# Layer 0's output projection turned into features by tokens, with a block-transposed way back for the residual

## The chip, the cores and the metric

The kernel runs on one core of one Trainium2 chip. The core has TensorE (PE in the profile, with its weight loads shown apart as PEld), VectorE (DVE), ScalarE (ACT), GpSimd (POOL) and SyncE (SP). Here SP issues nearly all transfers, and POOL a few. The metric is the device time of one execution in microseconds. The kernel before takes 2053.34 us, the median of three runs (2053.01, 2053.34 and 2054.17 us).

## The reference

The program is a two-layer encoder over 256 tokens of 2048 features, in float32. In each layer 12 mixing heads and 4 heads that look into 256 memory tokens run side by side. Their outputs are concatenated (16 heads of 128, "cat") and go through one output projection, whose result is added to the residual. A squared-ReLU MLP of width 8192 follows. Every sub-layer normalises its input first.

```
h = x
for i in range(DEPTH):
    n = rms_norm(h, attn_norm[i])
    ...
    h = h + jnp.concatenate([mix, cross], axis=-1) @ w_o[i]
    n = rms_norm(h, mlp_norm[i])
    h = h + jnp.square(jax.nn.relu(n @ w_up[i])) @ w_down[i]
return rms_norm(h, final_norm)
```

The change touches the line with `w_o[0]`, and what carries its result into the norm behind it and into the residual.

## The kernel before

**Products.** Every float32 operand is split into a rounded high part and the rest (`split`, L299: ScalarE writes the high part, VectorE the low part), and each product is three TensorE products: high by high, high by low, low by high. There are two forms. In form "S" (`s_products`, L215) a 128x128 block of weights is stationary and the 256 tokens stream past; the result has features on partitions and tokens along the row. In form "M" (`m_products`, L202) 128 tokens of the activation are stationary and 512 columns of weights stream past; the result has tokens on partitions. Layer 0's query and key projections and both up projections (`u_products`, L690) have the first form. The value projections, all of layer 1's input projection and both output projections have the second.

**Weights.** A chunk of weights is 128x2048 (1 MB), loaded by SP into one of three "raw" slots. It is split in two halves into `hi` and `lo` tiles, of which there are four each, so a half can be split once the half four before it has been multiplied. The up projection has its own set on the side: two raw slots (`raw_U`) and two slots each of `uh` and `ul`.

**The output projection** (`add_o`, L674) goes over four blocks of 512 output features. Each needs four chunks, whose rows are heads: 12 to 15 (memory heads), 0 to 3, 4 to 7, 8 to 11. Blocks 0 and 1 are interleaved so that heads 8 to 11, the last to be ready, come last. `o_done` (L603) adds a block to `h` (tokens by features) and sums squares. After three of the four blocks `guard` forms a scale from them, so the up projection need not wait for the full norm; its inverse (`inv`) corrects what the MLP adds to `h`. Then `scaled` (L621) multiplies `h` by the scale, and `transposed` (L314) turns it to features by tokens on TensorE: 32 transposes of 128x128 (L319), each feature tile then split into `hT` (`split_pair`, L324). The up projection multiplies with `hT`.

**Order.** The author writes a list of half-chunks ("grains"). Each has a run, and loads and splits a few grains ahead; `later(n, ...)` puts a piece of work n grains later. The framework then orders the instructions of every engine itself: it takes this order as a priority and goes by its own estimate of when data will be there. The order is fixed when the program is built. Each engine, and SP and POOL as issuers of transfers, then works through its list strictly in order: a row that waits holds up all rows behind it.

Of the kernel before, what the change touches and what calls it, by code (L numbers as in the profile page):

```python
# [57 lines left out]
class Work:  # L58


    def __init__(self, kind, src, acts, first, begins, last, start, done):
        self.kind, self.src, self.acts = kind, src, acts
        self.first, self.begins, self.last, self.start, self.done = first, begins, last, start, done
        self.early = False


# [8 lines left out]
def encoder_kernel(ctx: ExitStack, tc: tile.TileContext, t: dict, out: bass.AP):  # L75
# [69 lines left out]
    def halves_of(w):  # L145
# [9 lines left out]
        def prep(hf):  # L155
            if hf == 0:
                tiles["raw"] = at.ring.tile([P, CH], F32, tag="raw", bufs=3, name="raw")
                nc.sync.dma_start(tiles["raw"], w.src)
            tiles[hf] = new_half(w.kind)
            split(*tiles[hf], tiles["raw"][:, hf * HALF : (hf + 1) * HALF])  # L160
# [54 lines left out]
    def s_products(w, k0, nk, hi, lo):  # L215

        acts, ps = w.acts(), w.ps[:, :SEQ]
        for j in range(nk):
            k = k0 + j
            s = slice(j * P, (j + 1) * P)  # L220
            nc.tensor.matmul(ps, hi[:, s], acts[:, k, :SEQ], start=k == 0, stop=False)  # L221
            nc.tensor.matmul(ps, hi[:, s], acts[:, k, SEQ:], start=False, stop=False)  # L222
            nc.tensor.matmul(ps, lo[:, s], acts[:, k, :SEQ], start=False, stop=k == KT - 1)  # L223

# [121 lines left out]

    def attend(qT, kT, bias=None):
        sc_ps = at.att.tile([P, NT, SEQ], F32, tag="att", name="sc_ps")
# [20 lines left out]
        for s in range(NT):  # L369
            nc.vector.tensor_scalar(sc[:, s, :], sc[:, s, :], rs[:, s : s + 1], None, op0=ALU.mult)  # L370
        return sc
# [18 lines left out]

    def attention(jobs, at, gap=1, lag=1):

        def step(n, job, prev):
            qT, kT, bias, v, head, cat = job
            if n == 0:
                res = attend(qT, kT, bias)
# [120 lines left out]
    def x_stats():  # L517
# [6 lines left out]
        box["x_col"] = keep.tile([P, NT], F32, name="x_col")  # L524
        nc.vector.tensor_copy(box["x_col"], rstd_of(ss, D, "x"))
        box["x_row"] = at.work.tile([P, SEQ], F32, tag="x_row", bufs=1, name="x_row")
        along_free(box["x_col"], box["x_row"])
# [27 lines left out]
    def a_k_done(hd):  # L555
        def f(w):
            k = at.work.tile([P, 512], F32R, tag="b_y2", name="kT")
            s = summed(w.ps, "k", box["x_row"])
            split(k[:, :SEQ], k[:, SEQ:], s)
            b = at.work.tile([P, BJ * GRID_W], F32, tag="b_o", bufs=3, name="bias")  # L560
            nc.sync.dma_start(b, t["bias"][hd])
            attention([(box.pop(("q", hd)), k, b, head_of(box["v", hd // GH], hd % GH), hd, box["cat"])], 1)
        return f

    def a_qm_done(hd):
        def f(w):
# [4 lines left out]
            split(q[:, :SEQ], q[:, SEQ:], s)  # L571
            attention([(q, box["km"][:, hd, :], None, head_of(box["vm"], hd), NH + hd, box["cat"])], 1)
        return f
# [29 lines left out]
    def o_done(layer, nb):  # L603
# [33 lines left out]
        def f(w):  # L637
# [20 lines left out]
            if nb == 3:  # L658
# [7 lines left out]
                later(6, past, squares)  # L666
                later(8, past, inv)
        return f

# [312 lines left out]

    add_o(0)
    add_mlp(0)
# [246 lines left out]
```

## Time and profile before

| | |
|---|---|
| median of three runs | 2053.34 us |
| span of the profiled execution | 2050.6 us |
| median less span | 2.7 us |
| PE busy | 2028.0 us (99%) |
| DVE, ACT busy | 1657.1 us (81%), 1242.0 us (61%) |
| output projection of layer 0 | 347.6 to 440.4 us of the span, its last transposes to 444.4 us |
| up projection of layer 0 begins | 440.5 us |

The page does not state the profiled execution's whole time; its span is compared with the median of the runs. In the rows, a time stamp counts from the span's start. Products overlap, so their durations (0.28 or 0.39 us each) do not add up to time; the distance from one start to the next does.

### The profile page before, as it was taken

To read this page: it belongs to the slowest core of one execution; us is meant where nothing else is said; L and a number is where in the kernel's file an instruction comes from. 1 tells how busy PE (TensorE), PEld (TensorE's weight loads), DVE (VectorE), ACT (ScalarE), POOL (GpSimd) and SP (SyncE) were. 2 spreads that over 40 slices of the span, in tenths; PEclk is the share of its full clock that TensorE was granted. 3 is DMA by queue.
4 is the path that set the end of the run, shared out by engine and by line. 5 is a ranking of instruction groups with operands and counts; after the bars stand their busy time and mean duration, and the time that the engine had idled before them with its cause. 6 is when DMAs were issued, how large, how long until landed. Compare 5 with 4: busy or idle time off the path is not lost.

```text
span 2050.6 us, 32620 instructions
## 1 busy us (share of the span) xinstructions
PE 2028.0 (99%) x13092; PEld 1835.2 (89%) x13092; DVE 1657.1 (81%) x2025; ACT 1242.0 (61%) x1616; POOL 120.2 (6%) x144
## 2 busy tenths in 40 slices
PE   8999999999999999999999999999999999999998
PEld 7899999889999999999988888889999999999996
DVE  6766666558998999989896667657989999999896
ACT  6645454556666666666655557556666666666664
POOL 0000000000000000000000001000000000000000
PEclk9999999999999999999999999999999999999999
DMA  7755555727777777777765554537878787777773
GB/s 280 284 190 180 189 175 178 275 86 224 234 228 232 218 238 230 220 234 226 232 219 204 178 180 144 195 115 224 242 223 237 215 243 220 232 226 228 231 220 134
DMA packets 93431, 433.84 MB, mean 212 GB/s; under 512 B 10464, under 2 KB 12128, under 8 KB 60128
## 3 DMA queue, kind: packets, MB, share of 16 engines
q1 hardware_dynamic: 75888, 399.25, 57.7%
q0 software_dynamic: 16816, 31.46, 8.7%
q8 instruction: 102, 1.67, 0.3%
q10 hardware_dynamic: 576, 1.05, 0.1%
q14 instruction: 49, 0.40, 0.1%
HBM read 398.17 MB, written 4.19 MB: 196 GB/s over the span
## 4 chain that ended last, share of the span: by engine, by line
PE 94%; DVE 3%; DMA 1%; ACT 1%; issue 1%; SPq 0%; POOLq 0%; POOL 0%; DVEq 0%; ACTq 0%
PE ps_u L698 11%; PE ps_u L696 11%; PE ps_u L697 11%; PE p L810 8%; PE p L811 8%; PE p L812 8%; PE ps_m L209 8%; PE ps_m L212 8%; PE ps_m L213 8%; PE ps_s L221 3%; PE ps_s L223 3%; PE ps_s L222 3%; DVE ul L302 1%; PE pt_a L378 1%; DVE tl L302 1%
## 5 line engine op out<-in xcount | busy, mean ns | idle before, releaser
L698 PE MATMUL ps_u<-hT,ul 128*128 128x256 f32 x2048 | 568.1, 278 | 2.4 <-DVE ul L302 2.3
L696 PE MATMUL ps_u<-hT,uh 128*128 128x256 f32 x2048 | 568.0, 277 | 0.1
L697 PE MATMUL ps_u<-hT,uh 128*128 128x256 f32 x2048 | 567.4, 277 | 0.0
L301 ACT ACTIVATE uh<-raw_U 128x1024 fp32r<-128x1024 f32 x278 | 294.6, 1061 | 303.5 <-PE ps_u L697 281.0
L302 DVE TENSOR_TENSOR lo<-raw,hi 128x1024 fp32r<-128x1024 f32 (+1 forms) x224 | 266.3, 1195 | 162.1 <-ACT hi L301 160.0
L698 PEld LDWEIGHTS ps_u<-hT,ul 128*128 128x128 f32 x2048 | 385.5, 188 | 5.2 <-DVE ul L302 4.2
L696 PEld LDWEIGHTS ps_u<-hT,uh 128*128 128x128 f32 x2048 | 384.9, 188 | 5.5 <-ACT uh L301 0.5
L697 PEld LDWEIGHTS ps_u<-hT,uh 128*128 128x128 f32 x2048 | 384.4, 188 | 4.6
L302 DVE TENSOR_TENSOR ul<-raw_U,uh 128x1024 fp32r<-128x1024 f32 x278 | 337.2, 1218 | 37.5 <-ACT uh L301 37.4
L301 ACT ACTIVATE hi<-raw 128x1024 fp32r<-128x1024 f32 (+1 forms) x224 | 231.8, 1040 | 215.9 <-PE ps_m L213 121.1
L301 ACT ACTIVATE th<-t 128x2048 fp32r<-128x2048 f32 x112 | 215.2, 1921 | 125.4 <-PE p L812 111.8
L302 DVE TENSOR_TENSOR tl<-t,th 128x2048 fp32r<-128x2048 f32 x112 | 256.1, 2286 | 26.4 <-ACT th L301 25.8
L302 DVE TENSOR_TENSOR bl<-b,bh 128x1536 fp32r<-128x1536 f32 x112 | 196.0, 1750 | 0.3 <-ACT bh L301 0.2
L811 PE MATMUL p<-tl,a_s 128*128 128x512 f32 x448 | 177.2, 395 | 0.0
L812 PE MATMUL p<-th,a_s 128*128 128x512 f32 x448 | 174.4, 389 | 0.0
L301 ACT ACTIVATE bh<-b 128x1536 fp32r<-128x1536 f32 x112 | 166.2, 1484 | 10.1 <-PE p L812 4.0
L810 PE MATMUL p<-th,a_s 128*128 128x512 f32 x448 | 166.1, 395 | 0.0
L790 POOL DMA_DIRECT2D t<-b x112 | 97.1, 867 | 1166.0 <-DVE t L789 593.6
L811 PE MATMUL p<-bl,a_s 128*128 128x512 f32 x336 | 131.0, 390 | 0.2 <-DVE bl L302 0.2
L812 PE MATMUL p<-bh,a_s 128*128 128x512 f32 x336 | 131.1, 390 | 0.0
L789 DVE TENSOR_TENSOR t<-t,b 128x512 f32<-128x512 f32 x112 | 77.2, 689 | 64.1 <-DMA t<-in_w_pair 52.5
L223 PE MATMUL ps_s<-nT,lo 128*128 128x256 f32 x448 | 124.9, 279 | 0.0
(233 smaller groups left out, 3813.4 us busy)
## 6 DMA issues: line engine op xcount, KB each, us to landing
raw_U<-in_w_up SPq DMA_DIRECT2D x128, 1024.0 KB, 6.6
b<-in_w_pair SPq DMA_DIRECT2D x112, 768.0 KB, 4.5
raw<-in_w_o SPq DMA_DIRECT2D x32, 1024.0 KB, 5.1
t<-in_w_pair SPq DMA_DIRECT2D x112, 256.0 KB, 3.5
t<-b POOLq DMA_DIRECT2D x112, 256.0 KB, 6.8
raw<-in_w_b SPq DMA_DIRECT2D x21, 1024.0 KB, 5.0
raw<-in_w_av SPq DMA_DIRECT2D x12, 1024.0 KB, 5.1
raw<-in_w_aq SPq DMA_DIRECT2D x12, 1024.0 KB, 5.0
```

The costliest lines, as they stand in the source:

```text
L209: first = nc.tensor.matmul(w.ps[i], ah, hi[:, s], start=st, stop=False)
L212: nc.tensor.matmul(w.ps[i], ah, lo[:, s], start=False, stop=False)
L213: nc.tensor.matmul(w.ps[i], al, hi[:, s], start=False, stop=sp)
L223: nc.tensor.matmul(ps, lo[:, s], acts[:, k, :SEQ], start=False, stop=k == KT - 1)
L301: first = nc.scalar.activation(dst_hi, src, AF.Copy)
L302: return first, nc.vector.tensor_tensor(dst_lo, src, dst_hi.bitcast(F32), op=ALU.subtract)
L696: nc.tensor.matmul(ps, hi[:, s], acts[:, k, :SEQ], start=k == 0, stop=False)
L697: nc.tensor.matmul(ps, hi[:, s], acts[:, k, SEQ:], start=False, stop=False)
L698: nc.tensor.matmul(ps, lo[:, s], acts[:, k, :SEQ], start=False, stop=k == KT - 1)
L810: nc.tensor.matmul(ps, a[:, 0, ai, :], hi[:, s], start=begins, stop=False)
L811: nc.tensor.matmul(ps, a[:, 0, ai, :], lo[:, s], start=False, stop=False)
L812: nc.tensor.matmul(ps, a[:, 1, ai, :], hi[:, s], start=False, stop=ends)
```

## The change

Layer 0's output projection becomes form S (`add_o_still`): 16 works, one per tile of 128 output features, each with one chunk of weights `w_os` whose 16 blocks are in the order of heads 12 to 15, 0 to 11. The first four works are interleaved: their four first halves, then their four second halves. The result has features on partitions, as the up projection needs it.

The scale now comes from the input instead of three blocks of `h`: the probabilities of all layer 0 heads are multiplied by the reciprocal root of the mean square of `x` of their token (`factor`, an extra operand of an instruction that is there already), so `cat` carries it, and the projection's result comes out scaled. `rows` loads `x` once more, features by tokens (four loads of 512 KB, `x_s`), and multiplies it by the same scale. For each feature tile VectorE adds the two into `room`, and `split_pair` makes `hT` of it.

`h` itself has to be tokens by features for the MLP's additions. For every pair of feature tiles `back` transposes 32x32 blocks on VectorE (one instruction for 128x512), writes them to DRAM in four transfers on SP (64 KB each, `turn`), and reads them back in one transfer on POOL (256 KB). Five grains later `landed` copies them on ScalarE into `h`, times the inverse scale, and after every second pair sums the squares.

Besides, `raw` has four slots for three, and the framework's scratch memory for transfers issued by POOL is set to 8192.

```diff
-    raws = [at.ring.tile([P, CH], F32, tag="raw", bufs=3, name=f"raw{c}") for c in range(FIRST_CHUNKS)]
+    raws = [at.ring.tile([P, CH], F32, tag="raw", bufs=4, name=f"raw{c}") for c in range(FIRST_CHUNKS)]
...
+                nc.vector.tensor_scalar(sc[:, s, :], sc[:, s, :], rs[:, s : s + 1], factor[:, i : i + 1],
+                                        op0=ALU.mult, op1=ALU.mult)
...
+    def add_o_still(layer):
+
+        heads = [*range(NH, KT), *range(NH)]
+        works = []
+        for n in range(KT):
+            def start(w):
+                w.ps = at.acc.tile([P, 512], F32, tag="acc", name="ps_s")
+            works.append(Work("S", t["w_os"][n], get("cat"), 0, True, True, start, o_still_done(layer, n)))
+            works[-1].kts = heads
+        first = [halves_of(w) for w in works[:4]]
+        for hf in range(2):
+            plan.extend(x[hf] for x in first)
+        plan.extend(works[4:])
+
+    def o_still_done(layer, n):
+
+        def back():
+            room = box["room"]
+            x, y, z = (room[:, i, :] for i in range(3))
+            nc.vector.transpose(y.rearrange("p (b i d r) -> p d i b r", b=4, i=2, d=2),
+                                x.rearrange("p (d i b j) -> p d i b j", d=2, i=2, b=4))
+            f = P
+            turn = dram.tile([P, 4, f], F32, tag="turn", bufs=4, name="turn")
+            to = turn.rearrange("(b r) a f -> a r b f", r=32)
+            for a in range(4):
+                nc.sync.dma_start(to[a], y.rearrange("p (b f) -> p b f", b=4)[32 * a : 32 * a + 32])
+            z = z.rearrange("p (a f) -> p a f", a=4)
+            nc.gpsimd.dma_start(z, turn)
+            later(5, landed, z, n // 2)
+
+        def landed(z, pair):
+            src = z.rearrange("p a (i d r) -> p i d a r", i=2, d=2)
+            for i in range(NT):
+                dst = h[:, i, pair * 256 : (pair + 1) * 256].rearrange("p (d a r) -> p d a r", d=2, a=4)
+                nc.scalar.activation(dst, src[:, i], AF.Copy, scale=box["x_root"][:, i : i + 1])
+            if pair % 2:
+                for i in range(NT):
+                    sum_squares(2 * layer, i, pair // 2)
+            if pair == KT // 2 - 1:
+                inv()
...
+        def rows(q):
+            x = at.side.tile([P, 3 * 512], F32, tag="b", bufs=2, name="x_s")[:, : 4 * SEQ]
+            nc.sync.dma_start(x, t["xT"][:, q * 4 * SEQ : (q + 1) * 4 * SEQ])
+            x = x.rearrange("p (a b) -> p a b", b=SEQ)
+            nc.vector.tensor_tensor(x, x, box["x_row"][:, None, :].to_broadcast([P, 4, SEQ]), op=ALU.mult)
+            box["x_s", q] = x
+
+        def f(w):
+            if n == 0:
+                closed("work")
+                at.side = opened("side", side="right")
+                box["hT"] = wide(f"hT{layer}")
+                rows(0)
+            if n % 4 == 0 and n < 12:
+                rows(n // 4 + 1)
+            if n % 2 == 0:
+                box["room"] = at.side.tile([P, 4, 512], F32, tag="T", bufs=2, name="room")
+            x = box["room"][:, 0, n % 2 * SEQ : n % 2 * SEQ + SEQ]
+            nc.vector.tensor_tensor(x, w.ps[:, :SEQ], box["x_s", n // 4][:, n % 4, :], op=ALU.add)
+            split_pair(box["hT"], x, (G_M0, G_M1)[layer], n)
+            if n % 2:
+                back()
+        return f
...
-    add_o(0)
+    add_o_still(0)
...
-    nc = _bacc.Bacc("TRN2", target_bir_lowering=False, num_devices=1)
+    nc = _bacc.Bacc("TRN2", target_bir_lowering=False, num_devices=1, dynamic_dma_scratch_size=8192)
```

**How the order moves.** Line numbers in the changed program are those of the changed file (L223 to L225 are the three products of form S, L303 and L304 the two parts of `split`). On PE, as the second halves of the first four works begin to end, the changed program has these rows. `ps_s_3876`, `3915`, `3953` and `3982` are the sums of works 0 to 3, and `hi_3949`, `hi_3978`, `hi_4007` and `hi_4050` are the high parts of their second halves:

```order
L224 MATMUL ps_s_3982<-cat0_1142,hi_4050 128x256
L223 MATMUL ps_s_3876<-cat0_1142,hi_3949 128x256
L223 MATMUL ps_s_3915<-cat0_1142,hi_3978 128x256
L223 MATMUL ps_s_3953<-cat0_1142,hi_4007 128x256
L225 MATMUL ps_s_3982<-cat0_1142,lo_4051 128x256
L223 MATMUL ps_s_3982<-cat0_1142,hi_4050 128x256
L224 MATMUL ps_s_3876<-cat0_1142,hi_3949 128x256
L225 MATMUL ps_s_3876<-cat0_1142,lo_3950 128x256
L224 MATMUL ps_s_3915<-cat0_1142,hi_3978 128x256
L225 MATMUL ps_s_3915<-cat0_1142,lo_3979 128x256
L224 MATMUL ps_s_3953<-cat0_1142,hi_4007 128x256
```

The last three products of works 0, 1 and 2, those of head 11, stand behind five products of work 3's second half; until then the sums and the weight tiles of all three stay in use. VectorE has, in that stretch, the following rows. The first row holds the low parts of the second halves of works 2 and 3, and the later `lo` rows are the halves of work 4:

```order
L304 TENSOR_TENSOR lo<-raw,hi 128x1024 x2
L304 TENSOR_TENSOR pT<-pt_a,pT 128x512
L304 TENSOR_TENSOR cat_1142<-av,cat_1142 128x256
L736 TENSOR_TENSOR x_s<-x_s,x_row 128x1024
L750 TENSOR_TENSOR room<-ps_s,x_s 128x256 x3
L736 TENSOR_TENSOR x_s<-x_s,x_row 128x1024
L304 TENSOR_TENSOR lo<-raw,hi 128x1024
L702 STREAM_TRANSPOSE room<-room 128x2x2x4x32
L304 TENSOR_TENSOR lo<-raw,hi 128x1024
```

Both multiplications of `x_s`, and three additions that wait for head 11, stand ahead of the split of work 4's first half. At the other end, where the up projection of layer 0 begins, ScalarE had these rows before:

```order
L301 ACTIVATE uh<-raw_U 128x1024
L327 ACTIVATE hT_4327<-pt_n,gains 128x256 x4
L586 ACTIVATE sq,ssq_114<-h 128x512
L301 ACTIVATE uh<-raw_U 128x1024
L586 ACTIVATE sq,ssq_114<-h 128x512
L301 ACTIVATE uh<-raw_U 128x1024
L750 ACTIVATE c<-ps_u 128x256
```

In the changed program it has these, where the first row of L717 is the sixth of `landed` counted from zero (features 1536 to 1791), the second is the last, and `uh` rows are halves of up chunks 1, 1, 2 and 2:

```order
L329 ACTIVATE hT_4039<-room,gains 128x256 x2
L717 ACTIVATE h<-room,x_root 128x256 x2
L329 ACTIVATE hT_4039<-room,gains 128x256
L303 ACTIVATE uh<-raw_U 128x1024 x2
L836 ACTIVATE c<-ps_u 128x256
L837 ACTIVATE c<-c 128x256
L717 ACTIVATE h<-room,x_root 128x256 x2
L599 ACTIVATE sq,ssq_114<-h 128x512
L303 ACTIVATE uh<-raw_U 128x1024
L599 ACTIVATE sq,ssq_114<-h 128x512
L303 ACTIVATE uh<-raw_U 128x1024
```

The copy of the last pair back into `h`, which reads a transfer from DRAM, now stands ahead of the split of up chunk 2. SP, the issuer, has at that place:

```order
L159 DMA raw<-in_w_os 128x2048
L861 DMA b<-in_w_pair 128x1536
L708 DMA turn<-room 32x4x128 x8
L863 DMA t<-in_w_pair 128x512
L861 DMA b<-in_w_pair 128x1536
L708 DMA turn<-room 32x4x128 x4
L794 DMA raw_U<-in_w_up 128x2048
L863 DMA t<-in_w_pair 128x512
L794 DMA raw_U<-in_w_up 128x2048 x5
```

The four writes of the last pair stand behind the MLP's first load `t`, which takes the memory of the sixth pair's `room` and so waits until that pair has been copied into `h`. Before, SP had two `t` and six `raw_U` in a row there, and no writes.

More of the change, by code (lines that the diff above doesn't have):

```diff
@@ L64, in __init__ @@
         self.early = False
+        self.kts = range(KT)
 class Grain:
@@ L156, in prep @@
             if hf == 0:
-                tiles["raw"] = at.ring.tile([P, CH], F32, tag="raw", bufs=3, name="raw")
+                tiles["raw"] = at.ring.tile([P, CH], F32, tag="raw", bufs=4, name="raw")
                 nc.sync.dma_start(tiles["raw"], w.src)
@@ L369, in attend @@
         for s in range(NT):
-            nc.vector.tensor_scalar(sc[:, s, :], sc[:, s, :], rs[:, s : s + 1], None, op0=ALU.mult)
+            if factor is None:
+                nc.vector.tensor_scalar(sc[:, s, :], sc[:, s, :], rs[:, s : s + 1], None, op0=ALU.mult)
+            else:
+                i = NT - 1 - s
+                nc.vector.tensor_scalar(sc[:, s, :], sc[:, s, :], rs[:, s : s + 1], factor[:, i : i + 1],
+                                        op0=ALU.mult, op1=ALU.mult)
         return sc
@@ L389, in attend3, with attention @@
         split(cat[:, head, :SEQ], cat[:, head, SEQ:], av[:, :SEQ])
-    def attention(jobs, at, gap=1, lag=1):
+    def attention(jobs, at, gap=1, lag=1, factor=None):
         def step(n, job, prev):
@@ L395, in step @@
             if n == 0:
-                res = attend(qT, kT, bias)
+                res = attend(qT, kT, bias, factor)
             elif n == 1:
@@ L524, in x_stats @@
         box["x_col"] = keep.tile([P, NT], F32, name="x_col")
-        nc.vector.tensor_copy(box["x_col"], rstd_of(ss, D, "x"))
-        box["x_row"] = at.work.tile([P, SEQ], F32, tag="x_row", bufs=1, name="x_row")
+        box["x_mean"] = keep.tile([P, NT], F32, name="x_mean")
+        nc.vector.tensor_scalar(box["x_mean"], ss, 1.0 / D, EPS, op0=ALU.mult, op1=ALU.add)
+        nc.gpsimd.tensor_tensor(box["x_col"], box["x_mean"], mhalf[:, :NT], op=ALU.pow)
+        box["x_root"] = keep.tile([P, NT], F32, name="x_root")
+        nc.vector.tensor_tensor(box["x_root"], box["x_mean"], box["x_col"], op=ALU.mult)
+        box["x_row"] = keep.tile([P, SEQ], F32, name="x_row")
         along_free(box["x_col"], box["x_row"])
@@ L561, in f @@
             nc.sync.dma_start(b, t["bias"][hd])
-            attention([(box.pop(("q", hd)), k, b, head_of(box["v", hd // GH], hd % GH), hd, box["cat"])], 1)
+            attention([(box.pop(("q", hd)), k, b, head_of(box["v", hd // GH], hd % GH), hd, box["cat"])], 1,
+                      factor=box["x_col"])
         return f
@@ L571, in f @@
             split(q[:, :SEQ], q[:, SEQ:], s)
-            attention([(q, box["km"][:, hd, :], None, head_of(box["vm"], hd), NH + hd, box["cat"])], 1)
+            attention([(q, box["km"][:, hd, :], None, head_of(box["vm"], hd), NH + hd, box["cat"])], 1,
+                      factor=box["x_col"])
         return f
@@ new lines, in o_still_done, with inv @@
+    def o_still_done(layer, n):
[22 more added lines that the diff above has]
+                inv()
+        def inv():
+            v = mean_square(2 * layer, 4, "full")
+            box["inv"] = keep.tile([P, NT], F32, tag="inv", name="inv")
+            nc.vector.reciprocal(v, v)
+            nc.vector.tensor_tensor(box["inv"], v, box["x_mean"], op=ALU.mult)
+            box["ninv"] = keep.tile([P, NT], F32, tag="ninv", name="ninv")
+            nc.vector.tensor_scalar(box["ninv"], box["inv"], -1.0, None, op0=ALU.mult)
+        def rows(q):
[19 more added lines that the diff above has]
+                back()
@@ L1214 @@
         arrays[f"w_vm{i}"] = m_chunks(a["w_mem_kv"][i][:, memw:])
-        arrays[f"w_o{i}"] = m_chunks(a["w_o"][i])
+        if i == 0:
+            rows = a["w_o"][i].reshape(KT, HD, D)
+            arrays["w_os"] = s_chunks(np.concatenate([rows[NH:], rows[:NH]]).reshape(D, D))
+        else:
+            arrays[f"w_o{i}"] = m_chunks(a["w_o"][i])
         arrays[f"w_up{i}"] = s_chunks(a["w_up"][i])
```

9 lines of the change are left out of this document (5 added, 4 removed).

## The prediction

> **What bounds the kernel now.** I read the page's engine shares first, then the stretches of the span around the projection and the start of the MLP, then who TensorE waited for there.
>
> ```profile
> PE 2028.0 (99%) x13092; PEld 1835.2 (89%) x13092; DVE 1657.1 (81%) x2025; ACT 1242.0 (61%) x1616; POOL 120.2 (6%) x144
> 347.00:450.00 103.00, 102.95 (x521) 87.28 (x519) 57.41 (x72) 53.53 (x81) 0.69 (x1) 1.00 0.49 181
> 447.00:451.00 4.00, 3.45 (x28) 3.05 (x27) 2.85 (x5) 2.85 (x7) 0.00 (x0) 1.00 0.01 2
> 451.00:475.00 24.00, 23.69 (x208) 23.69 (x209) 15.45 (x26) 14.16 (x21) 0.00 (x0) 1.00 0.57 188
> 475.00:490.00 15.00, 13.63 (x112) 13.02 (x111) 13.51 (x17) 11.29 (x14) 1.93 (x2) 1.00 0.81 245
> PE ps_u L698 <- DVE ul L302: 1.1, 2, 0.8
> 448.95 1.06 ACT uh L301
> 450.03 1.24 DVE ul L302
> ```
>
> In a row of stretches the numbers are the length, then the busy time of PE, PEld, DVE, ACT and POOL, then the granted clock. TensorE has no free time in the projection (102.95 of 103.00 us), at full clock. VectorE (57.4) and ScalarE (53.5) have nearly half of it free. So only two things can move the time: how long TensorE's own list is, and waits that the new rows put into it. Before, it waits 0.8 us at the first split of up chunk 1's second half (the chain shows `uh`, then `ul`), and 1.4 us (15.00 less 13.63) where the first down products begin. The second belongs to code that the change leaves.
>
> **TensorE's list.** The same multiplications in the two forms:
>
> ```profile
> 343.04 0.28 PE L223 MATMUL ps_s<-nT,lo 128*128 128x256 f32 x1
> ...
> 347.46 0.28 PE L223 MATMUL ps_s<-nT,lo 128*128 128x256 f32 x1
> 400.14 0.39 PE L212 MATMUL ps_m<-lo,cat 128*128 128x512 f32 x1
> ...
> 402.86 0.39 PE L213 MATMUL ps_m<-hi,cat 128*128 128x512 f32 x1
> 425.01 0.22 PE pt_n L319 x2
> 425.47 1.53 PE pt_n L319 x14
> 435.42 0.87 PE pt_n L319 x8
> 442.59 0.22 PE pt_n L319 x2
> 443.75 0.66 PE pt_n L319 x6
> ```
>
> From 343.04 to 347.46 us lie 39 products of form S: 0.1133 us each. From 400.14 to 402.86 lie 12 of form M: 0.2267 us. Form M has 16 k-blocks x 2 token tiles x 4 feature blocks x 3 = 384 products, 87.0 us. Form S has 16 x 16 x 3 = 768, also 87.0 us. **That term is zero.** What goes is the 32 transposes: the five rows of the chain add up to **3.5 us**. The 26 small products of heads 10 and 11 that fall into the stage stay.
>
> **Start of the stage.** Count from A, the first product of the projection. A half is 24 products, 2.72 us. The small products are spaced about 0.12 us:
>
> ```profile
> 353.94 0.28 PE L386 MATMUL av<-pT,va 128*128 128x256 f32 x1
> 355.61 0.39 PE L209 MATMUL ps_m<-hi,cat 128*128 128x512 f32 x1
> L302 DVE TENSOR_TENSOR lo<-raw,hi 128x1024 fp32r<-128x1024 f32 x30 | 36.6, 1224 | 28.5 <-ACT hi L301 28.4
> L301 ACT ACTIVATE hi<-raw 128x1024 fp32r<-128x1024 f32 x29 | 30.7, 1060 | 32.4 <-PE ps_m L213 28.0 <-PE ps_s L222 1.7 <-issue 1.4
> L343 DVE SCALAR_TENSOR_TENSOR k_s<-ps_s,x_row 128x256 f32<-128x256 f32 x1 | 0.4, 425 | 0.5 <-PE ps_s L223 0.5
> ```
>
> (14 pieces in 1.67 us there, so 26 take 3.1 us.) By the order on PE, works 0 to 2 end after 4x24 + 3x21 + 5 + about 3 = 167 products: A + 18.9 + 3.1 = A + 22.0. Work 4 is due 25 products later, A + 24.9, and needs its low part two products on, A + 25.1. From A + 22.0 VectorE has three additions (3 x 0.425), one multiplication of `x_s` (128x1024, 1.22 as a split of that size) and the split (1.22): A + 25.7, **0.6 us late** even with all data there. The first `x_s` stands on SP behind the eighth weight chunk, whose slot is free when the low part of work 3's second half is split: work 3's first half ends at A + 13.7 (96 products and most of the small ones), plus 1.06 and 1.22, A + 16.0.
>
> ```profile
> raw<-in_w_o SPq DMA_DIRECT2D x3, 1024.0 KB, 5.0
> raw<-in_w_o SPq DMA_DIRECT2D x5, 1024.0 KB, 8.4
> t<-in_w_pair SPq DMA_DIRECT2D x1, 256.0 KB, 3.2
> 380.00:390.00 10.00, 10.00 (x46) 8.28 (x45) 5.94 (x6) 4.82 (x6) 0.00 (x0) 1.00 1.01 406
> ```
>
> The chunk lands 5.0 us later, at A + 21.0, and 0.5 MB behind it at 406 GB/s takes 1.3 more: A + 22.3. Then 1.22 + 1.28 + 1.22 + 1.22 end at A + 27.2, 2.1 us late. With an uncrowded 3.2 us it stays 0.6; with the crowded chunk of 8.4 us it is 5.5. I take **1.5**, since the nearest row (5.0) points to 2.1 and smaller transfers to 0.6.
>
> **The way back.** For each pair: a transpose (nearest row: an addition of 128x512, 0.69), four issues, a write, a return on POOL, two copies.
>
> ```profile
> L789 DVE TENSOR_TENSOR t<-t,b x3: 685/685/692, 475.3 to 494.0; 128x512 f32<-128x512 f32 x3
> 375.03 0.33 SPq L158 DMA_DIRECT2D raw<-in_w_o  x1
> gains<-in_gains SPq DMA_DIRECT2D x1, 40.0 KB, 1.9
> mem_k<-km_w SPq DMA_DIRECT2D x4, 256.0 KB, 9.6
> t<-b POOLq DMA_DIRECT2D x1, 256.0 KB, 3.7
> t<-b POOLq DMA_DIRECT2D x112, 256.0 KB, 6.8
> L586 ACT ACTIVATE sq<-h 128x512 bf16<-128x512 f32 x8 | 5.0, 624 | 3.1 <-DVE h L644 3.1
> L586 ACT ACTIVATION_READ_ACCUMULATOR sq<-h 128x1 f32 x7 | 1.3, 187 | 0.0
> ```
>
> A write of 64 KB lies between 1.9 (40 KB) and 9.6 (256 KB into DRAM in a crowded stretch); I take 2.3, near the small one, for no weights are moving then. The return lies between 3.7 and 6.8; I take 3.7, the one of the quiet stretch. From the transpose's start that is 0.7 + 4x0.33 + 2.3 + 3.7 = 8.0 us. For pairs 0 to 6 this is hidden: weights are split three halves (8.2 us) ahead, a split takes 2.3, so ScalarE may stand still for 5.9 us before TensorE sees it, and each copy stands at least one pair (10.9 us) behind its sums. Not hidden is pair 7. Count from B, the first up product: its last addition ends at B + 0.65, its return lands at B + 8.7. ScalarE, in order, then copies twice (0.42 each, as L343's size), squares once (0.62 + 0.19) and makes the high part of up chunk 2 (1.06), VectorE the low part (1.22): B + 12.6. Chunk 2 is due after 96 products, B + 10.9, its low part at B + 11.1: **1.5 us of waiting**. Below, 1.9 for the write gives 1.1, and a prompt start of the copies nothing. Above, 9.6 and 6.8 give 1.5 + 7.3 + 3.1 = 11.9.
>
> [...]
>
> **What else changes costs nothing:** 16 additions of 128x256, 8 transposes and 4 multiplications on VectorE are some 17 us (16 x 0.425, 8 x 0.69, 4 x 1.22), against 8 additions of 128x512 that go (5.5), and lie in the 45 us that it has free; were it full instead, TensorE would wait for all 12; the second scalar in `factor` rides on an instruction that stays; the fourth `raw` slot lets loads go earlier where TensorE is already full. The old 0.8 us wait goes: both halves of chunk 0 are split long before, and ScalarE has chunk 1 next.
>
> **Sum:** -3.5 - 0.8 + 1.5 + 1.5 = -1.3. The span goes from 2050.6 to 2049.3 us; the median stands 2.7 us above the span, so **2052.0 us**.
>
> **Rivals.**
>
> *The waits stay out* (24%). Transfers land as the quick rows say and the order holds: start of stage 0.6 or less, way back 0. Then -3.5 - 0.8 + 0 to 0.6, so 2049.0 to 2049.6, a little more if the rebuilt order also closes one of the other small gaps (the 1.4 us at the first down products). For it: VectorE and ScalarE are half idle. Against it: both waits come from rows that stand in order ahead of a split, not from load.
>
> *ScalarE stands behind the last return* (14%, the other side). Place: the copy of pair 7 ahead of chunk 2's split. The write stands on SP behind the MLP's `t`, which waits for pair 6's copy, so a late return is paid twice: pair 6 late by d delays pair 7's write too. With 9.6 and 6.8 the wait is 11.9 us, and pair 6 (10.9 us earlier, 8.0 + 10.4 us long) adds about 6: net -4.3 + 1.5 + 18 = +15, 2068 us; a middle case (3 us on each leg) is +1.5 + 6 + 1.5 - 4.3 = about +5, 2058 us. It decides from a return that lands later than about B + 14. Against it: the stretch is quiet (0.01 of DMA at 447 to 451 us before).
>
> *A product of half the columns is not half as dear* (4%). Form S loads weights twice as often, and a product could cost its weight load rather than its columns. PEld shows 188 ns for one; if that set the pace, 768 x 0.188 = 144 us, 57 more: 2110 us. Against it: the products of `ps_s` above are of this form, with the same loads, and stand 0.1133 us apart.
>
> ```profile
> L209 PEld LDWEIGHTS ps_m<-hi,cat 128*128 128x128 f32 x128 | 24.0, 188 | 4.9
> ```
>
> [...]
>
> **How the numbers follow.** A measurement of this kernel can tell about 0.2%, 4.1 us, from no change: 2049.2 to 2057.4 us. The forecast (58%) lies within; the first rival lies on the border and I count it as faster; the last two are slower. Likeliest 2052.0. Its own range is 2050 to 2056 (waits of 0.6 to 5.5 at the start, 0 to 3 at the end). To hold 8 in 10 it reaches to 2048.0 below and, with the middle case of the late return, to 2059.0 above. Faster 0.24, the same 0.58, slower 0.18.
>
> **What would show it.** In the profile of the changed kernel: 768 products of `ps_s` on `cat` at 0.113 us and no L319 in layer 0; TensorE idle some 1 to 2 us around work 4, released by VectorE's `lo`; idle again some 1 to 2 us at up chunk 2, released by `ul`, with ScalarE's L717 just ahead, released by the transfer from `turn`; the up projection beginning near 440. It would be wrong if TensorE waits elsewhere in the stage (for `cat` of head 11, for a late weight chunk behind a write on SP), or if a gap outside layer 0's projection moves by more than 1 us.

## The result, and the profile after

The changed kernel takes 2082.78 us (median of four runs, 2081.55 to 2083.71) against 2053.18 us of the kernel before in four runs: a ratio of 1.0145, with a 95% interval of 1.0133 to 1.0156. It is slower by 29.6 us where 2052.0 was forecast, and lies 24 us outside the range.

Half of that (5.0, 1.1 and 9.4 us) is lost in stages of which the change touches little (layer 0's norm and `factor` in its heads) or nothing, and nearly all the rest in the first MLP, of which it touches only the entrance. The table gives the length of each stage in the two profiled executions, from the first product that reads the stage's operand to the first of the next one:

| stage | before, us | after, us | difference |
|---|---|---|---|
| memory keys and values | 93.2 | 93.1 | -0.1 |
| layer 0, query, key and value projections and heads | 247.4 | 252.4 | +5.0 |
| layer 0, output projection | 92.9 | 92.4 | -0.5 |
| layer 0, MLP | 673.1 | 688.0 | +14.9 |
| layer 1, projections and heads | 148.6 | 149.7 | +1.1 |
| layer 1, output projection | 109.6 | 109.6 | 0.0 |
| layer 1, MLP | 669.6 | 679.0 | +9.4 |

First TensorE's line of the page and three stretches of the changed kernel: the first layer's projections, the middle of the first MLP and the middle of the second. A row has the length, then busy time and count of PE, PEld, DVE, ACT and POOL, then the granted clock.

```profile
PE 2051.9 (99%) x13444; PEld 1872.2 (90%) x13444; DVE 1670.6 (80%) x2041; ACT 1241.1 (60%) x1624; POOL 124.5 (6%) x151
111.00:340.00 229.00, 229.00 (x1668) 216.69 (x1667) 150.42 (x220) 113.80 (x186) 0.00 (x0) 1.00 0.51 175
600.00:1000.00 400.00, 400.00 (x2638) 366.50 (x2636) 363.50 (x393) 252.81 (x252) 32.71 (x38) 1.00 0.75 225
1500.00:1900.00 400.00, 399.74 (x2630) 365.84 (x2630) 361.88 (x390) 253.33 (x254) 32.61 (x38) 1.00 0.75 226
```

The same stretches of the kernel before:

```profile
111.00:340.00 229.00, 229.00 (x1709) 217.14 (x1708) 151.94 (x224) 115.63 (x188) 0.00 (x0) 1.00 0.53 179
600.00:1000.00 400.00, 400.00 (x2676) 365.74 (x2675) 367.00 (x398) 257.58 (x257) 34.02 (x39) 1.00 0.77 229
1500.00:1900.00 400.00, 400.00 (x2675) 365.88 (x2674) 369.09 (x401) 258.71 (x258) 33.44 (x39) 1.00 0.77 229
```

TensorE is busy nearly all the time (all but 0.3 us) at full clock in both, and yet fewer products get through: 1668 for 1709, 2638 for 2676, 2630 for 2675. A busy share of 100% hides this; the count beside it shows it. The products themselves take longer, as the groups of the stretch 600 to 1000 us show (the high by high products of the up projection, first of the kernel before, then of the changed one; the number behind the busy time is the mean duration in ns):

```profile
L696 PE MATMUL ps_u<-hT,uh 128*128 128x256 f32 x620 | 171.9, 277 | 0.0
```

```profile
L782 PE MATMUL ps_u<-hT,uh 128*128 128x256 f32 x611 | 171.7, 281 | 0.0
```

What sets the pace is the distance from one start to the next. Below, as in the table of the experiments, it is the mean over all pairs of records of a kind in the profiled execution that follow each other without a wait. In both kernels most of them lie near 113.3 ns or near 117.8. The up products (`u_products`) average 114.3 ns before and 117.5 after, the first layer's form S projections 114.8 and 118.6. The 768 products on `cat` that the change adds keep the fast step (113.5). In the changed kernel's timeline one wait shows both steps, with the same instructions in the same group:

```profile
493.84 0.28 PE L783 MATMUL ps_u<-hT,uh 128*128 128x256 f32 x1
...
494.90 0.28 PE L783 MATMUL ps_u<-hT,uh 128*128 128x256 f32 x1
495.15 0.38 PE L784 MATMUL ps_u<-hT,ul 128*128 128x256 f32 x1
...
495.84 0.28 PE L783 MATMUL ps_u<-hT,uh 128*128 128x256 f32 x1
...
497.88 0.28 PE L783 MATMUL ps_u<-hT,uh 128*128 128x256 f32 x1
```

From 493.84 to 494.90 us lie 9 steps of 117.8 ns; then comes one gap of 0.25 us, a short wait for `ul`, a step of 0.22 us and four more near 117.8; from 495.84 to 497.88 lie 18 steps of 113.3 ns. So the step is not a property of the instruction alone: the same product stands 117.8 ns behind the one before it, or 113.3, many times in a row. These two distances are what I call the slow and the fast step. That this gap is what changed the step, the rows do not show.

The waits that the prediction spoke of are there as well. In the changed kernel, whom TensorE waited for between 350 and 480 us (us in total, times, longest):

```profile
PE ps_u L782 <- ACT uh L303: 4.9, 1, 4.9
PE ps_s L225 <- DVE lo L304: 1.3, 1, 1.3
PE ps_u L784 <- DVE ul L304: 0.5, 1, 0.5
PE ps_s L223 <- ACT hi L303: 0.4, 1, 0.4
```

The last return in the changed kernel's timeline, on SP, POOL and ScalarE (start and duration in us; in brackets the idle time before and what ended it):

```profile
446.43 0.35 SPq L863 DMA_DIRECT2D t<-in_w_pair  x1
446.88 0.38 SPq L861 DMA_DIRECT2D b<-in_w_pair  x1
447.35 1.87 SPq L708 DMA_DIRECT2D turn<-room  x4
...
454.52 0.55 POOL L710 DMA_DIRECT2D room<-turn  x1 [11.34 <-DMA turn<-room]
...
458.21 0.91 ACT L717 ACTIVATE h<-room,x_root 128x256 f32<-128x256 f32 x2 [6.33 <-DMA room<-turn]
459.64 1.04 ACT L303 ACTIVATE uh<-raw_U 128x1024 fp32r<-128x1024 f32 x1
```

And its stretches around that, in the columns of above:

```profile
455.00:461.00 6.00, 1.10 (x9) 0.90 (x8) 0.29 (x1) 2.79 (x6) 0.07 (x1) 0.85 0.44 175
461.00:466.00 5.00, 4.53 (x20) 4.24 (x21) 3.41 (x10) 1.92 (x5) 0.00 (x0) 0.50 0.30 62
466.00:475.00 9.00, 9.00 (x78) 9.00 (x78) 4.88 (x5) 4.71 (x6) 0.00 (x0) 1.00 0.45 169
```

ScalarE stands before `landed` of the last pair until 458.21 us, and the split that TensorE needs comes behind it. During the 4.9 us of waiting the granted clock falls to 0.50, and in 461 to 466 us TensorE starts 20 products where some 42 fit at 0.118 us each.

### The profile page after: what moved, and what is told of

Read it like the earlier page. It is cut to its first block, busy times and chain, and to the rows that moved or that the text cites. A ratio compares the mean times of both kernels' runs of the same rounds, so it can differ in the third digit from the quotient of the medians.

```text
span 2079.6 us, 33441 instructions
## 1 busy us (share of the span) xinstructions
PE 2051.9 (99%) x13444; PEld 1872.2 (90%) x13444; DVE 1670.6 (80%) x2041; ACT 1241.1 (60%) x1624; POOL 124.5 (6%) x151
## 4 chain that ended last, share of the span: by engine, by line
PE 94%; DMA 2%; DVE 2%; ACT 1%; issue 1%; SPq 0%; POOLq 0%; POOL 0%; DVEq 0%; ACTq 0%
PE ps_u L784 11%; PE ps_u L782 11%; PE ps_u L783 11%; PE p L896 9%; PE p L898 8%; PE p L897 8%; PE ps_m L210 7%; PE ps_m L213 7%; PE ps_m L214 7%; PE ps_s L223 4%; PE ps_s L225 4%; PE ps_s L224 4%; PE pt_a L385 1%; DVE ul L304 0%; DMA room<-turn 0%
## 5 line engine op out<-in xcount | busy, mean ns | idle before, releaser
L782 PE MATMUL ps_u<-hT,uh 128*128 128x256 f32 x2048 | 575.9, 281 | 4.9 <-ACT uh L303 4.9
L784 PE MATMUL ps_u<-hT,ul 128*128 128x256 f32 x2048 | 576.3, 281 | 1.5 <-DVE ul L304 1.5
L783 PE MATMUL ps_u<-hT,uh 128*128 128x256 f32 x2048 | 575.7, 281 | 0.0
L303 ACT ACTIVATE uh<-raw_U 128x1024 fp32r<-128x1024 f32 x278 | 294.7, 1061 | 332.4 <-PE ps_u L783 312.1
L784 PEld LDWEIGHTS ps_u<-hT,ul 128*128 128x128 f32 x2048 | 392.0, 191 | 3.3 <-DVE ul L304 2.4
L304 DVE TENSOR_TENSOR lo<-raw,hi 128x1024 fp32r<-128x1024 f32 (+1 forms) x224 | 266.2, 1194 | 150.1 <-ACT hi L303 149.1
L304 DVE TENSOR_TENSOR ul<-raw_U,uh 128x1024 fp32r<-128x1024 f32 x278 | 338.0, 1220 | 50.0 <-ACT uh L303 49.4
L303 ACT ACTIVATE hi<-raw 128x1024 fp32r<-128x1024 f32 (+1 forms) x224 | 231.2, 1038 | 201.8 <-PE ps_m L214 97.9
L304 DVE TENSOR_TENSOR tl<-t,th 128x2048 fp32r<-128x2048 f32 x112 | 256.2, 2288 | 44.6 <-ACT th L303 44.3
L303 ACT ACTIVATE th<-t 128x2048 fp32r<-128x2048 f32 x112 | 215.0, 1920 | 126.4 <-PE p L898 114.6
L304 DVE TENSOR_TENSOR bl<-b,bh 128x1536 fp32r<-128x1536 f32 x112 | 196.1, 1751 | 0.3 <-ACT bh L303 0.2
L303 ACT ACTIVATE bh<-b 128x1536 fp32r<-128x1536 f32 x112 | 165.8, 1480 | 9.9 <-PE p L898 4.0
L224 PE MATMUL ps_s<-nT,hi 128*128 128x256 f32 x448 | 126.5, 282 | 0.0
L225 PE MATMUL ps_s<-nT,lo 128*128 128x256 f32 x448 | 126.4, 282 | 0.0
```

The lines of the kernel that those rows point to most:

```text
L303: first = nc.scalar.activation(dst_hi, src, AF.Copy)
L304: return first, nc.vector.tensor_tensor(dst_lo, src, dst_hi.bitcast(F32), op=ALU.subtract)
```

## The experiments

**What could have slowed the untouched stages.** The instructions of the second MLP, and their order on TensorE, are those of before. What the change does move is where tiles lie. `x_row` (1024 bytes) and two small columns now live until the MLP, the fourth `raw` slot adds 8192 bytes, the smaller scratch takes 8192 away. The programs' allocations give these addresses (bytes within a partition; "distance" is the address of the weights that TensorE loads next less that of the operand that streams, modulo 256):

```
                                    before    after
nT                                  34944     26752
hi of the attention stages, form S  93376     94464
   distance nT to hi                   64       128
hT                                  34464     26272
uh (layer 1)                       199648    199648
   distance hT to uh                   64        64
a_s, bh                    93312, 136320    86208, 129216
   distance hT to a_s (up to down)    224        32
   distance bh to a_s (down to down)    0         0
   distance bh to uh (down to up)      96        32
```

Within one stage the distance changes from product to product by multiples of 256. In the first layer's projections of the kernel before it is 64, 320, 576 or 832 modulo 1024, about equally often, and the step is 114.9, 115.0, 114.9 and 114.6 ns at these four; so a multiple of 256 changes it by no more than 0.4 ns there, and I count modulo 256.

Theory of places: the step depends on where operands lie. Rivals: the new waits throw TensorE out of step (the stream), or the small scratch does. Four kernels tell these apart.

`b_scr8` is the kernel before with one edit:

```diff
-    nc = _bacc.Bacc("TRN2", target_bir_lowering=False, num_devices=1)
+    nc = _bacc.Bacc("TRN2", target_bir_lowering=False, num_devices=1, dynamic_dma_scratch_size=8192)
```

> The kernel before with one edit: the descriptor scratch of GpSimd's DMAs is 8192 bytes instead of 16384, so that every tile on the left side of SBUF lies 8192 bytes lower (the operands hT and nT of the wide tiles at 26272 instead of 34464); every engine's order is the same and the right side (the up projection's weights uh, ul) stays. Theory of places (TensorE's 128x256 product takes 113 or 118 ns by where its two operands lie): the up products, whose two operands now lie 8192 bytes closer or farther, take about 117.5 ns instead of 114.3 on the mean, some 6144 x 3.2 ns = 20 us more, and the first layer's projections, whose operands moved together, stay at 247 us: 2062 to 2073 us. Rival of the stream (the changed order and its new waits throw TensorE out of step, whatever the places): 2053 us. Rival of the scratch (too few descriptors): longer POOL DMAs, and any time from 2055 up, in all stages.

Measured: 2052.86 us, ratio 0.9999 (0.9990 to 1.0008). The scratch is out. My guess that a distance of 8192 bytes matters is out too: up products at 114.7 ns.

`b_raw4` has that edit and `bufs=4` for `raw`.

> The kernel before with the scratch at 8192 bytes and a fourth buffer for raw weights, as in the change, and nothing else of the change: hT and nT lie 8192 bytes lower, the split weights of the attention stages and their other operands memT and cat stay where they were. Theory of places: up products some 20 us more as in the run with the scratch alone, and the first layer's projections may change too, since nT has moved against its weights: 2062 to 2078 us. Rival of the stream: 2053 us, or a little less by the earlier loads.

Measured: 2052.70 us, ratio 0.9993 (0.9984 to 1.0003). The fourth slot neither costs nor gains, and again a shift by a multiple of 256 bytes (8192) does nothing to the time.

`b_pad64` is the kernel before with an unused tile. All five engines have the same order as before.

```diff
     small = opened("small", bufs=3)
+    small.tile([P, 16], F32, tag="pad", bufs=1, name="pad")
```

> The kernel before with an unused tile of 64 bytes behind the small tiles: the split weights of the attention stages, memT and cat lie 64 bytes higher, nT, hT and the up projection's weights stay. In the change the distance from nT to its weights modulo 512 is 128 bytes where it was 64 before; here it becomes 128 as well. Theory of places, if it is the distance within 512 bytes that decides: the first layer's projections take about 118.6 ns a product in place of 115 and 252 us instead of 247, the up products stay: 2058 us. If only larger distances decide, or by the rivals of the stream and of the scratch: 2053 us.

Measured: **2076.56 us, ratio 1.0121 (1.0106 to 1.0136)**. 64 bytes cost 23.5 us. Its stretches, in the columns of above:

```profile
111.00:340.00 229.00, 229.00 (x1667) 216.65 (x1666) 148.78 (x220) 112.97 (x185) 0.00 (x0) 1.00 0.52 176
600.00:1000.00 400.00, 400.00 (x2638) 366.57 (x2637) 364.43 (x393) 254.07 (x254) 33.07 (x38) 1.00 0.76 226
```

These are the counts of the changed kernel (1668 and 2638) without anything of the change but the shift of 64 bytes modulo 256. Both expected times are missed by far. I had expected the first layer's projections to slow down (247.4 to 252.9 us, as measured), but not the up products, whose own operands do not move. The MLP's own tiles do move by 64 bytes here, and the distance from down to up becomes 32, as in the changed kernel.

`a_same_places` is the changed kernel with the addresses of before. `raw_room` is a helper that puts every fourth raw tile into a pool `low`, opened ahead of all others:

```diff
-        box["x_col"] = keep.tile([P, NT], F32, name="x_col")
-        box["x_mean"] = keep.tile([P, NT], F32, name="x_mean")
+        three = keep.tile([P, 3 * NT], F32, name="x_col")
+        box["x_col"], box["x_mean"], box["x_root"] = (three[:, i * NT : (i + 1) * NT] for i in range(3))
...
-        box["x_row"] = keep.tile([P, SEQ], F32, name="x_row")
+        box["x_row"] = h[:, NT - 1, D - SEQ :]
...
+        if rooms[0] % 4 == 0:
+            return low.tile([P, CH], F32, tag="raw", name="raw")
+        return at.ring.tile([P, CH], F32, tag="raw", bufs=3, name="raw")
```

> The changed kernel with the places of the kernel before: x_row lies in the last columns of h, which are free then, the three columns of x in one tile, and one of the four raw buffers ahead of the first tile, so that nT, hT, the attention stages' weights, memT and cat lie at the very bytes that they have before. The stages' work is that of the changed kernel. Theory of places: what the unchanged stages lost (5.0 us in the first layer's projections, 8.7 us in the second MLP, about 9 us in the first) is given back, the new waits at the stage's start and at the entrance of the MLP (about 7 us) stay: 2058 to 2064 us. Rivals of the stream and of the scratch: 2080 to 2084 us.

Measured: **2058.09 us, ratio 1.0025 (1.0015 to 1.0034)**, 24.7 us less than the changed kernel. Its stretches:

```profile
111.00:340.00 229.00, 229.00 (x1704) 217.09 (x1703) 153.49 (x224) 115.38 (x189) 0.00 (x0) 1.00 0.52 178
600.00:1000.00 400.00, 399.55 (x2674) 364.91 (x2673) 367.02 (x396) 255.72 (x256) 32.71 (x38) 1.00 0.75 227
```

TensorE's order is that of the changed kernel, and the counts are back near 1709 and 2676. The waits are still there (4.7 us at the MLP), so the rival of the stream falls with this run, and the theory of places stands.

**The wait at the MLP, and why up products slow down without moving.** `a_late` adds to `a_same_places` that ScalarE's copies of the last pair are queued behind later splits:

```diff
-            later(5, landed, z, n // 2)
+            later(7 if n == KT - 1 else 5, arrived, z, n // 2)
+
+        def arrived(z, pair):
+            if pair < KT // 2 - 1:
+                return landed(z, pair)
+            past(lambda: landed(z, pair), box["splits"][-1])
```

> The changed kernel at the places of the kernel before (as in the run a_same_places), and ScalarE's two copies of the last returned pair queued some seven grains later, behind the splits of the up projection's third to sixth halves. If the 4.7 us for which TensorE waits at the third half are ScalarE standing ahead of that split until the last return lands, they go, and nothing else changes: 2053 us (2052 to 2055). If the return itself is what is late, and its pair's sums or the loads that wait for its buffer are next, TensorE waits some us later in the same MLP: 2056 to 2058 us.

Measured: **2051.11 us, ratio 0.9992 (0.9983 to 1.0001)**, 7.0 us less than `a_same_places`, and 0.9 us below the expected range. All that TensorE still waits for between 350 and 480 us (its file has L223 to L225 as L232 to L234, and L303 and L304 as L312 and L313):

```profile
PE ps_s L234 <- DVE lo L313: 0.9, 1, 0.9
PE ps_s L232 <- ACT hi L312: 0.4, 1, 0.4
```

The stretches in which it was busy for 1.10 and 4.53 us in the changed kernel:

```profile
455.00:461.00 6.00, 6.00 (x53) 6.00 (x52) 4.00 (x5) 4.00 (x8) 0.00 (x0) 1.00 0.57 203
461.00:466.00 5.00, 5.00 (x45) 5.00 (x44) 3.31 (x11) 4.18 (x9) 0.00 (x0) 1.00 0.51 203
```

The wait was 4.7 us in `a_same_places`, so the gain is 2.3 us more than the wait. The granted clock is 1.00 in both stretches and no longer drops to 0.50: at that clock 26 products stood 0.213 us apart in `a_same_places` where 0.118 is usual, some 2.5 us.

`b_mlp64` is the kernel before with only the MLP's own tiles (`a_s`, `bh`, `th` and the like) 64 bytes higher:

```diff
                 at.mlp = opened("mlp")
+                at.mlp.tile([P, 16], F32, tag="pad", bufs=1, name="pad")
```

> The kernel before with the MLP's own tiles alone 64 bytes higher: neither operand of the up products moves (hT, uh, ul), nor any of the attention stages. The change from a down product to an up product then has the distance of 32 bytes modulo 256 that it has in the changed kernel. Theory of the carry-over (a product at a bad distance throws TensorE into the slow step, and the up products, at 64 bytes, stay in the step in which they begin): up products about 117.5 ns, 0.9 of them slow, some 19 us more, and the first layer's projections stay at 247 us: 2070 to 2074 us. Rival (a product's step depends on its own two operands alone): up products stay at 114.4 ns, and only the few products at the changes are longer: 2054 to 2056 us.

Measured: **2070.11 us, ratio 1.0087 (1.0073 to 1.0100)**. Its stretches:

```profile
111.00:340.00 229.00, 229.00 (x1709) 217.14 (x1708) 151.94 (x224) 115.64 (x188) 0.00 (x0) 1.00 0.52 179
600.00:1000.00 400.00, 400.00 (x2637) 366.46 (x2636) 364.57 (x395) 253.21 (x253) 33.14 (x38) 1.00 0.75 226
```

The first layer is untouched (1709) and the MLP as slow as in the changed kernel (2637), though `hT`, `uh` and `ul` have not moved: up products at 117.2 ns. The same group of 48 up products behind down products, its first, seventh and last product, in the kernel before and then in `b_mlp64`:

```profile
603.93 0.28 PE L696 MATMUL ps_u<-hT,uh 128*128 128x256 f32 x1
...
604.64 0.28 PE L696 MATMUL ps_u<-hT,uh 128*128 128x256 f32 x1
...
609.29 0.28 PE L698 MATMUL ps_u<-hT,ul 128*128 128x256 f32 x1
```

```profile
605.62 0.28 PE L696 MATMUL ps_u<-hT,uh 128*128 128x256 f32 x1
...
606.32 0.28 PE L696 MATMUL ps_u<-hT,uh 128*128 128x256 f32 x1
...
611.15 0.28 PE L698 MATMUL ps_u<-hT,ul 128*128 128x256 f32 x1
```

Before, six slow steps (118 ns) are followed by 41 of about 113.3; in `b_mlp64` the 41 stay at 117.8. So here the place of the down products' operands decides whether the 41 up products behind them come at 113.3 or at 117.8 ns. The rival, that only a product's own operands count, is refuted.

`a_tuned` and `b_mlp96` were meant to use this: 24 floats of pad instead of 16, on `a_late` and on the kernel before, and `uh` moved inside its tile where the MLP's last part streams it, to keep that distance to `a_p`:

```diff
-                own[c, hf] = half_of_side(own[0], hf, MOVING_AT)
+                own[c, hf] = half_of_side(own[0], hf)
```

> As a_late, with the MLP's own tiles 96 bytes higher, so that, modulo 256 bytes, the next weights lie 64 bytes behind the operand that streams wherever a 128x256 product is followed by a down product (they lay 224 behind), and 0 bytes behind where a down product is followed by an up product (96 before). If those are the distances at which TensorE keeps its fast step (113.3 and 226.7 ns), and if the up products' slow ones come only from being thrown out at these changes, the up products fall from 114.8 to about 113.4 ns, 6144 of them by 1.4 ns: 8 us less than a_late, 2045 us (2043 to 2049). If the slow ones have another cause: the same as a_late, 2053 us.

> The kernel before with the MLP's own tiles 96 bytes higher, as in a_tuned, and nothing else. If the distance modulo 256 bytes decides and carries over: up products from 114.4 to about 113.4 ns, 6 us less: 2047 us (2045 to 2050). Otherwise 2053 us.

Measured: 2060.51 us (ratio 1.0041, 1.0028 to 1.0053) and 2060.71 us (1.0041, 1.0027 to 1.0054). Both expectations missed, in the other direction: the down products became fast throughout (227.0 ns; 229.8 before), and the up products slow (117.1 and 116.9). My rule, that a change at a "fast" distance keeps the up products fast, was wrong.

**A row of shifts.** `a_left96` moves, modulo 256 bytes, only `a_s` (a pad of 24 floats ahead of the tiles `a` and one of 40 behind them); `a_mlp32`, `a_mlp128`, `a_mlp160`, `a_mlp192` and `a_mlp224` are `a_late` with that many bytes of pad as in `b_mlp64`.

> a_late with only the left operands of the down products (a_s, a_p: the weights that TensorE loads) 96 bytes higher; the streamed sides (bh, bl, th, tl) keep their places modulo 256 bytes. Distances from the streamed operand to the next weights: 64 where an up product is followed by a down product (224 before), 96 from down product to down product (0 before), 96 from down to up product (as before). In the runs so far the up products were quick where they were entered at 96, and the down products where they were entered at 64. If the entry decides and 96 is a quick distance for products of 512 columns: down products 227 ns in place of 229.4 on the mean, 2350 of them by 2.5 ns, and up products no worse: 2043 to 2047 us. If 96 is slow for products of 512 columns, they take 229 to 233 ns and the up products 117.5: 2055 to 2075 us.

> a_late with the MLP's own tiles 32 bytes higher: 0 from up to down product, 64 from down to up product. By the table of the runs so far 0 is slow for products of 256 columns and 64 for those of 512, so both entries are bad: up products about 117.5 ns, 18 us more than a_late, 2066 to 2072 us. If only the distance at which a product itself stands counts: 2051 us.

> a_late with the MLP's own tiles 128 bytes higher: 96 from up to down product, 224 from down to up product. If places count modulo 128 bytes, nothing changes: 2051 us. If they count modulo 256 bytes, the entries differ from a_late and the time does: up products slow at 224, 2060 to 2070 us, or, if 224 is a quick entry, 2043 to 2050 us.

> a_late with the MLP's own tiles 192 bytes higher: 160 at both changes, a distance at which no product has stood yet. No theory gives its side: if 160 is a slow entry, 2066 to 2072 us as at 64 bytes higher; if it is quick, 2040 to 2050 us.

> a_late with the MLP's own tiles 160 bytes higher: 128 from up to down product, 192 from down to up product, between the two quick ones (128 and 192 bytes higher). If the entry from the down product into the up products decides and every slow change from 96 to 224 leaves them quick: 2044 to 2048 us. If each distance is for itself: up to 2068 us.

> a_late with the MLP's own tiles 224 bytes higher: 192 from up to down product, 128 from down to up product. By the same rule (changes at 96 to 224 leave the up products quick, changes at 0 to 64 slow): 2044 to 2050 us; otherwise 2060 to 2068 us.

Measured, with the means of the steps in ns (up products have 256 columns, down products 512):

| kernel | up to down | down to down | down to up | up step | down step | time, us | ratio to before |
|---|---|---|---|---|---|---|---|
| a_late | 224 | 0 | 96 | 114.6 | 229.8 | 2051.11 | 0.9992 |
| a_mlp32 | 0 | 0 | 64 | 117.7 | 228.3 | 2064.30 | 1.0052 |
| a_tuned (96) | 64 | 0 | 0 | 117.1 | 227.0 | 2060.51 | 1.0041 |
| a_mlp128 | 96 | 0 | 224 | 114.2 | 228.2 | 2045.76 | 0.9965 |
| a_mlp160 | 128 | 0 | 192 | 117.5 | 227.1 | 2062.87 | 1.0050 |
| a_mlp192 | 160 | 0 | 160 | 113.9 | 228.9 | 2045.59 | 0.9964 |
| a_mlp224 | 192 | 0 | 128 | 117.2 | 227.5 | 2061.83 | 1.0046 |
| a_left96 | 64 | 96 | 96 | 113.9 | 234.0 | 2059.78 | 1.0032 |

The row separates two things. A product's own distance counts: down products that stand at 96 take 234.0 ns, at 0 from 227.0 to 229.8. And how TensorE enters the up products counts: fast up products come with down to up distances of 96, 160 and 224 bytes, slow ones with 0, 64, 128 and 192 (and with 32 in `b_mlp64`). `a_mlp128` rules out a period of 128 bytes (0.9965 of before, where `a_late` has 0.9992). The rule expected of `a_mlp160` and `a_mlp224`, that all changes from 96 to 224 are good, falls with both, and `a_mlp32` came out 2 us below its range. Why the odd multiples of 32 but one are good is not settled; I have no mechanism that gives it.

Places alone do not settle the step either. Up to the first MLP `a_late` and `a_left96` are the same program at the same addresses, yet in one profiled execution each the products on `cat` averaged 113.8 and 117.2 ns. They part at the wait for work 4's first half, which both have (0.4 and 0.9 us, 0.4 and 1.1 us); from there to the stage's end one is fast and the other slow. First `a_late`, then `a_left96`:

```profile
375.00:435.00 60.00, 60.00 (x532) 60.00 (x531) 45.34 (x60) 36.02 (x58) 3.51 (x6) 1.00 0.72 247
```

```profile
375.00:435.00 60.00, 60.00 (x512) 60.00 (x511) 44.57 (x58) 36.08 (x58) 3.50 (x6) 1.00 0.71 244
```

The stage takes 92.3 and 95.0 us, so 2.7 us of what `a_left96` lost does not come from its shift.

`a_mlp192` and `a_mlp128` beat both kernels (intervals 0.9952 to 0.9977 and 0.9952 to 0.9979). Whether that belongs to the places alone:

> The kernel before with the MLP's own tiles 192 bytes higher and nothing of the change. If the gain of a_mlp192 over a_late (5.5 us) comes from the places alone, it comes here too: 2047 us (2046 to 2049). If the places are worth less without the change's other edits: 2051 to 2053 us.

Measured: 2049.87 us, ratio 0.9984 (0.9976 to 0.9993), between the two ranges expected, so places alone give 2.7 us. The change with its own best places gives 7.3 us (2045.59 against 2052.93 on its chip), so what the change itself does is worth some 4 to 5 us there, and 1.6 us at the old places (2051.11 against 2052.71), where the interval still holds no gain at all. Why it is worth more at the new places is open: the steps of `b_mlp192` are as quick as those of `a_mlp192` (113.5 and 228.9 ns).

## Why the prediction was wrong

The miss is 2082.78 - 2052.0 = 31 us. By the runs, the change's 29.6 us are 24.7 (places: changed kernel less `a_same_places`) + 7.0 (the last return: `a_same_places` less `a_late`) - 2.1 (the rest: `a_late` less before; against the runs of before on its own chip it is 1.6). Each part is the difference of two kernels in a row, so that they must add up.

**The step that failed: "What else changes costs nothing".** It went through instructions one by one, and for the fourth `raw` slot asked only when loads go. It never asked what the new tiles do to the addresses of all others. Its signs of being wrong looked for gaps, and most of the loss lies in no gap. The kernel's own text had a hint: constants `STILL_AT = 64` and `MOVING_AT = 160` that set where operands start inside their tiles. The 1088 bytes of `x_row` and two columns, 64 modulo 256, cost 24.7 us, nearly all in stages that the prediction took as fixed.

**TensorE's list: right.** Two of the new products in the changed kernel's timeline:

```profile
439.83 0.28 PE L225 MATMUL ps_s<-cat,lo 128*128 128x256 f32 x1
...
444.25 0.28 PE L225 MATMUL ps_s<-cat,lo 128*128 128x256 f32 x1
```

39 steps in 4.42 us, 0.1133 us each, and no transposes of layer 0. The rival of a half-width product that is not half as dear named the right quantity for the wrong reason: it looked at the new products and at the time of a weight load, while the dearer ones were old and only 4% dearer.

**Start of the stage: right.** 1.3 and 0.4 us of waiting, released by `lo` and `hi`, against 1.5. The rows came as counted: the first `x_s` was there 22.7 us after the stage's start (22.3 forecast), the split of work 4 ended at 27.4 (27.2).

**The way back: right place, wrong size.** The return was to take 3.7 us and took 3.7 (454.5 to 458.2). The write was to take 2.3, "for no weights are moving then". For the last pair they were: SP issued `t` and `b`, 1 MB, just ahead of it, since `t` had waited for the pair before. The four writes took 5.6 us in the median; those of the pair before, with nothing ahead, 1.8. The issues of the changed kernel in three windows (446 to 450, 439 to 442, 454 to 455 us), with KB each and the median us to landing:

```profile
b<-in_w_pair SPq DMA_DIRECT2D x1, 768.0 KB, 6.3
t<-in_w_pair SPq DMA_DIRECT2D x1, 256.0 KB, 4.4
turn<-room SPq DMA_DIRECT2D x4, 64.0 KB, 5.6
...
turn<-room SPq DMA_DIRECT2D x4, 64.0 KB, 1.8
room<-turn POOLq DMA_DIRECT2D x1, 256.0 KB, 3.7
```

So the 1.5 us were 4.9 and 0.5, the larger released by `uh` and not by `ul`, and a term was missing behind them: the half clock. This is the rival of ScalarE behind the last return in its middle case (+6 on the wait), which the prediction priced without the clock at 2058 us; `a_same_places` measures it at 2058.1. That the two agree is in part luck: the waits there are 4.7 and 0.7 us where that case has 7.5, and the half clock makes up for it.

**The sum.** Without places and with the last return out of the way, `a_late` shows -1.6 us where -1.3 was forecast. That agreement owes something to chance: its MLP wait is 0 and not 1.5, and its up products are 0.23 ns slower than before (6144 of them, 1.4 us).

## What to carry to other kernels

When a change adds or resizes a tile that lives long, compare the addresses of the operands of the products in all later stages, modulo 256 bytes, before and after (64 bytes cost 23.5 us in `b_pad64`); and when a time moves in stages that a change does not touch, count products in a stretch that is 100% busy, and move one pad by 64 bytes, before looking for waits. Put a copy that waits for a round trip through DRAM behind the next splits on its engine, not ahead of them (7.0 us less in `a_late`). Price a wait on TensorE as long as those at the MLP, 4.9 and 4.7 us, with the half clock that came with them: 6.8 us at 0.50 in the changed kernel, some 2.5 us of loss in `a_same_places`.

## What the runs showed of the hardware

- **A product's step depends on where its operands lie.** 64 bytes of shift, with all orders the same, took the products that start in 111 to 340 us from 1709 to 1667 and cost 23.5 us in all (`b_pad64`). In the changed kernel, with 1668 there, the first layer's 128x256 products stand 118.6 ns apart, before 114.8. Why the place of one operand against the other counts, no run shows.
- **A step goes on over many products.** Behind the same six slow steps, 41 up products whose own operands had not moved came at 113.3 ns before and at 117.8 in `b_mlp64`. At an unchanged distance of 64 they averaged 113.5 ns in `b_mlp192`, with 160 from down to up product, and 117.7 in `a_mlp32`, with 64. In the stage of the products on `cat`, at the same addresses and behind the wait that both have, 532 products started from 375 to 435 us in `a_late` and 512 in `a_left96`. What keeps the step no run shows.
- **A wait of 4.9 us halved the clock.** In the changed kernel the granted clock was 0.50 from 459.2 to 466.1 us, 6.8 us long; it fell 3.4 us after the last product and was back 5.3 us after the next one began. In `a_same_places`, with a wait of 4.7 us, the half clock was as long, but it fell 5.0 us after the last product, when TensorE had just begun again. In `a_late`, without the wait, it stayed at 1.00 from 455 to 475 us. The prediction's rival had waits of up to 18 us and priced no half clock.
